# More feed-forward pairs multiplied by blocks, with their weight chunks declared up front

## The chip, the cores and the metric

One Trainium2 chip, one of its cores. The metric is the device time of one execution of the kernel, in microseconds (us). Smaller is better. Inputs lie in HBM in fp32, the output is written there in fp32.

## The reference, cut to what matters

Two layers work on 512 tokens of width 1024. In each, a modulated RMSNorm feeds two parallel branches (chunkwise retention and causal pooling), whose gated sum is projected and added to x. Then comes the feed-forward, which the change touches:

```python
mod = c_act @ w_ada[l] + b_ada[l]
sh1, sc1, g1, sh2, sc2, g2 = jnp.split(mod, N_MOD, axis=-1)
...
h2 = modulate(rmsnorm(x, norm2[l]), sh2, sc2)
gate, up = jnp.split(h2 @ w_ffn_in[l], 2, axis=-1)      # 1024 -> 2 x 2816
x = x + g2[:, None, :] * ((jax.nn.silu(gate) * up) @ w_ffn_out[l])
```

## The kernel before, in words

**Layout.** Activations are kept transposed: 128 features on the partitions, 512 tokens along the free axis. A weight unit is a block of 128x128; eight units make a chunk of 128x1024 fp32 (512 KB), the unit of loading, laid out in HBM in the order of use. A product of fp32 accuracy is made of three matmuls (`mm3`): both operands are split into a high part rounded to fp32r and a low part, the rest; high by high, low by high and high by low are summed in PSUM.

**Weight chunks.** `prep(c)` makes an ordinary chunk ready. SyncE's queue (SP) loads it into one of three `raw` tiles; `copy` writes the high part into a `w` tile, on ScalarE or VectorE; the low part goes into a second `w` tile, in one of two ways. Either VectorE or GpSimd subtracts (`nc.either`), or, for the chunks that `is_added` names, ScalarE writes the negated high part and a DMA from GpSimd's queue loads the chunk a second time and accumulates it there. There are 11 `w` tiles.

**Feed-forward.** The 2816 hidden columns are 22 tiles of 128. A *pair* i is gate tile i and up tile i: 16 units, two chunks. An ordinary pair takes 2 x 8 x 3 = 48 matmuls of 128x512. A pair *by blocks* (`seven`) treats the product as 2x2 blocks (halves of the contraction, halves of the tokens, gate and up) and makes it of seven block products in place of eight: 84 matmuls of 128x256, of the same three terms. It needs sums of blocks of the activations (tiles `x`, made once a layer) and of the weights (`seven_prep`, for each chunk): four VectorE operations of 128x256 into two kept `r` tiles, a high and a low part of 128x768 of the chunk itself, and a high and a low part of 128x512 of each of the two sums, in four `w` tiles together. Its four PSUM banks are then put together by five VectorE operations and one on ScalarE, ahead of silu, the product with up, and the split of the hidden tile. Pairs 0 to 10 are followed by a first half of `ffn_out` (11 hidden tiles), pairs 11 to 21 by the second half, where x is closed for the next norm. `background()` fetches one tile of `w_ada` (512 KB) and reduces it on VectorE, once for each ordinary pair.

**What sets the order.** The code only records operations (`Recorder.add`, so all carry the line L421). `Recorder.order` then gives each an engine, where there is a choice, and a place, from modelled costs and due times counted back from TensorE's fixed order; the engines run what it wrote down, in order. Tiles `raw`, `w` and `ps` are handed out strictly in the recorded order.

**Looking ahead.** `ahead(c)` (called for each unit) prepares chunks c to c + 2. A chunk found in the dictionary `sevens` goes to `seven_prep`, any other to `prep`. Before the change a chunk enters `sevens` only in `seven_chunk`, when its pair's turn has come. By then the look-ahead of the pair ahead has already put both chunks through `prep`; they are loaded and prepared once more by `seven_prep`, and what `prep` made of them is read by nobody. The table `SEVEN` names pairs 5, 7, 9, 11, 13, 15, 17 and 19 of each layer, so that 32 chunks are loaded twice.

Of the kernel before, what the change touches and what calls it, by code (L numbers as in the profile page):

```python
# [17 lines left out]
DEPTH = 2  # L18
# [8 lines left out]
FT = FF // P  # L27
FF_CUTS = (0, 11, FT)
EPS = 1e-6
PAD = 16  # L30
UNITS = 8
# [31 lines left out]
STAT_TILES = {"out": 4, "ffn_out": 3}  # L63
STAT_AT = 2

SEVEN = [set(range(5, FT - 1, 2))] * DEPTH
HALF_KT = KT // 2


# [363 lines left out]
def trunk(ctx, tc, xT, cin, wada, vecs, wst, rot, trid, icnt, out):  # L433


    nc = Recorder()
# [5 lines left out]
    def ps():  # L442
        return nc.tile(pp, [P, S], F32, "ps", 8)
# [7 lines left out]
    def keep(dt=F32R):  # L451
        return nc.tile(ap, [P, S], dt, "r", N_ROW)

    def weights():
        return nc.tile(wp, [P, UNITS * P], F32R, "w", N_W)

    def raw_tile():
        return nc.tile(wp, [P, UNITS * P], F32, "raw", N_RAW)
# [41 lines left out]
    order = {}  # L500
# [21 lines left out]
    sevens = {}  # L522

    def seven_chunk(l, i, k0):
        c = len(order) // UNITS
        assert len(order) % UNITS == 0
        for k, col in ((0, 0), (HALF_KT, 0), (HALF_KT, FF), (0, FF)):
            for d in range(2):
                order[(l, "ffn_in", k + k0 + d, col + i * P)] = len(order)
        sevens[c] = None  # L530
        return c

    def seven_prep(c):

        if sevens[c] is not None:
            return
        w = 2 * P
        af = raw_tile()
        nc.sync.dma_start(out=af, in_=wst[c])
        ah, al, sh, sl = (weights() for _ in range(4))  # L540
        a11, a12, a22, a21 = (af[:, n * w:n * w + w] for n in range(4))
        s34, s21 = keep(F32), keep(F32)
        nc.vector.tensor_sub(out=s34[:, :w], in0=a21, in1=a11)
        nc.vector.tensor_add(out=s21[:, :w], in0=s34[:, :w], in1=a22)
        nc.vector.tensor_add(out=s21[:, w:], in0=a21, in1=a22)
        nc.vector.tensor_sub(out=s34[:, w:], in0=a12, in1=s21[:, :w])
        copy(ah[:, :3 * w], af[:, :3 * w])
        nc.either.tensor_sub(out=al[:, :3 * w], in0=af[:, :3 * w], in1=ah[:, :3 * w].bitcast(F32))
        for n, sf in enumerate((s34, s21)):
            part = slice(n * S, n * S + S)  # L550
            copy(sh[:, part], sf)
            nc.either.tensor_sub(out=sl[:, part], in0=sf, in1=sh[:, part].bitcast(F32))
        sevens[c] = (ah, al), (sh, sl)

    def unit(l, name, k, col, n=1):
        key = (l, name, k, col)
        if key not in order:
            for q in range(n):
                order[(l, name, k, col + q * P if n > 1 else col)] = len(order)
        c, o = divmod(order[key], UNITS)  # L560
        ahead(c)
        sl = slice(o * P, (o + n) * P)
        return his[c][:, sl], los[c][:, sl]

    def ahead(c):
        for cc in range(c, c + look[0] + 1):
            if cc in sevens:
                seven_prep(cc)
            else:
                prep(cc)  # L570

    def mm3(out_ap, w, a, start, stop):

        (wh, wl), (ah, al) = w, a
        for n, (s, m) in enumerate(((wh, ah), (wl, ah), (wh, al))):
            nc.tensor.matmul(out_ap, lhsT=s, rhs=m, start=start and n == 0, stop=stop and n == 2)

    def copy(out, src):
        nc.add({"scalar": ("copy", (), dict(out=out, in_=src)), "vector": ("tensor_copy", (), dict(out=out, in_=src))})
# [7 lines left out]
    def hs(h, sl):  # L587
        return tuple(z[:, sl] for z in h)
# [87 lines left out]
    def make_h(l, which, k, sl, h, whole=None):  # L676

        hh, hl = (z[:, sl] for z in h)
        sh = mods[l][:, (0 if which == 1 else 24) + k:][:, :1]
        t = temp()[:, sl]  # L680
        nc.vector.scalar_tensor_tensor(
            out=t, in0=x[k][:, sl], scalar=gains[l, which][:, k:k + 1], in1=rs[:, sl], op0=ALU.mult, op1=ALU.mult)
        nc.add({
            "scalar": ("activation", (hh, t, AF.Identity), dict(bias=sh)),
            "vector": ("tensor_scalar", (), dict(out=hh, in0=t, scalar1=sh, scalar2=None, op0=ALU.add)),
        })
        if whole is not None:
            nc.add({
                "scalar": ("activation", (whole, t, AF.Identity), dict(bias=sh)),
                "vector": ("tensor_scalar", (), dict(out=whole, in0=t, scalar1=sh, scalar2=None, op0=ALU.add)),  # L690
            })
        nc.vector.scalar_tensor_tensor(
            out=hl, in0=t, scalar=sh, in1=hh.bitcast(F32), op0=ALU.add, op1=ALU.subtract)
# [4 lines left out]
    def first_tiles(l, which, h, name, cols, norm_b, whole=lambda k, half: None):  # L698

        o = [ps() for _ in cols]  # L700
        for sl in (A, B):
            for k in range(KT):
                for t, c in zip(o, cols):
                    mm3(t[:, sl], unit(l, name, k, c), hs(h[k], sl), k == 0, k == KT - 1)
                if sl is A and k == STAT_AT:
                    norm_b()
                    for kk in range(KT):
                        make_h(l, which, kk, B, h[kk], whole(kk, 1))
        return o
# [148 lines left out]
    for l in range(DEPTH):  # L858
# [36 lines left out]
        for g in range(2):  # L895
# [33 lines left out]
            for i in range(4):  # L929
# [4 lines left out]
                for j in range(4):  # L934
                    c0 = min(j, 2) * P
                    w = S - c0
# [94 lines left out]

        while len(order) % UNITS:
            order[("none", len(order))] = len(order)
        done = first_tiles(l, 2, h2, "ffn_in", [0, FF, P], norm_b, block)
        for k in range(HALF_KT):
            t13, t24 = temp(), temp()
# [10 lines left out]
        def seven(i):  # L1047

            cs = [seven_chunk(l, i, k0) for k0 in (0, 2)]
            o = [ps() for _ in range(4)]  # L1050
            for k in range(HALF_KT):
# [29 lines left out]
        for f, (i0, i1) in enumerate(zip(FF_CUTS, FF_CUTS[1:])):  # L1081
            hid = []
            for i in range(i0, i1):
                if i in SEVEN[l]:
                    hid.append(seven(i))
# [114 lines left out]
```

## Time and profile before

| | |
|---|---|
| median of 3 runs | 1537.04 us (1536.17 to 1537.6) |
| the profiled execution's own time | 1535.18 us |
| its span, from first to last instruction | 1533.0 us |
| granted TensorE clock, mean | 0.995 |
| DMA packets | 286.77 MB, mean 187 GB/s |
| first layer's feed-forward pairs, TensorE | 421 to 536 us (0 to 10), 596 to 712 us (11 to 21) |
| second layer's | 1167 to 1285 us, 1346 to 1461 us |

How to read what follows: PE is TensorE, PEld its weight loads, DVE VectorE, ACT ScalarE, POOL GpSimd. In a row of a group, `out<-in` names tiles without buffer numbers, then come shape, count, busy time in us, the mean length of one in ns, and the idle time of the engine ahead of it with what ended it. In a row of the timeline the first two numbers are the start and the length in us; rows that follow each other with the same operation are merged. In a row of the windows the stretch and its length are followed by each engine's busy time (and count), then the granted clock, the DMA share and GB/s. `h` and `x` as the first input of a matmul are activations and their block sums, `r` in `ffn_out` the hidden tiles, `w` the weights, `t` temporaries.

### The profile page before, as it was taken

Reading aid. Unit: us, or ns where it says so; the run is one execution under the profiler, and the core shown is the slowest. Engines: PE = TensorE matmul, PEld = TensorE weight load, DVE = VectorE, ACT = ScalarE, POOL = GpSimd, SP = SyncE. Lnnn points to the kernel's source line nnn. Section 1 sums busy time; section 2 is a strip of 40 time slices with the busy share of each in tenths; the row PEclk is TensorE's granted clock in tenths of the full one; section 3 lists DMA queues with packets and bytes.
Section 4 is the critical chain, followed back from the end, with each engine's and each line's share of the span. In section 5 each row is a group of like instructions: output and inputs, shape, how many; then the busy total and the mean of one; then the engine's idle time right before and its main releaser. Section 6 shows DMA issues by size and latency. Waiting matters only on the chain. (4 is left out here: it accounts for less than half of the span.)

```text
span 1533.0 us, 20526 instructions
## 1 busy us (share of the span) xinstructions
PE 1503.3 (98%) x7878; PEld 1287.2 (84%) x7878; DVE 1006.4 (66%) x1650; ACT 645.7 (42%) x912; POOL 300.5 (20%) x291
## 2 busy tenths in 40 slices
PE   7999999999999999999999999999999999999997
PEld 5788888888888888998888888888889888899887
DVE  8877684465568957885366768535647696478633
ACT  2377552322464412342267766322227433243332
POOL 0023151011142300222011312101211432012101
PEclk8999999999999999999999999999999999999999
DMA  7857738789694684559487865777897757444553
GB/s 259 269 158 190 161 74 255 190 246 283 149 234 153 200 251 158 170 169 279 118 221 166 202 149 134 201 180 230 251 232 182 203 167 218 124 130 159 165 125 83
DMA packets 82788, 286.77 MB, mean 187 GB/s; under 512 B 9217, under 2 KB 11521, under 8 KB 82690
## 3 DMA queue, kind: packets, MB, share of 16 engines
q1 hardware_dynamic: 64114, 217.82, 42.5%
q0 software_dynamic: 18576, 67.64, 25.1%
q8 instruction: 61, 1.00, 0.3%
q14 instruction: 37, 0.30, 0.1%
HBM read 283.33 MB, written 2.10 MB: 186 GB/s over the span
## 5 line engine op out<-in xcount | busy, mean ns | idle before, releaser
L421 PE MATMUL ps<-h,w 128*128 128x512 f32 (+1 forms) x3888 | 793.4, 362 | 8.6 <-DVE h L421 5.2
L421 PEld LDWEIGHTS ps<-h,w 128*128 128x128 f32 x3888 | 659.1, 189 | 126.2 <-DVE h L421 6.4
L421 PE MATMUL ps<-r,w 128*128 128x512 f32 (+1 forms) x2430 | 476.8, 356 | 0.1
L421 PEld LDWEIGHTS ps<-r,w 128*128 128x128 f32 x2430 | 402.3, 188 | 69.1 <-DVE r L421 0.9
L421 ACT CAST w<-raw 128x1024 fp32r<-128x1024 f32 (+2 forms) x181 | 183.3, 1013 | 346.9 <-DMA raw<-wst 190.3
L421 DVE TENSOR_TENSOR w<-raw,w 128x1024 fp32r<-128x1024 f32 (+2 forms) x162 | 206.4, 1276 | 102.5 <-PE ps L421 71.7
L421 POOL DMA_DIRECT2D w<-wst x129 | 113.6, 881 | 743.6 <-ACT w L421 690.8
L421 ACT ACTIVATE w<-w 128x1024 fp32r<-128x1024 f32 x129 | 136.6, 1060 | 200.6 <-issue 75.6
L421 DVE CAST w<-raw 128x1024 fp32r<-128x1024 f32 (+2 forms) x115 | 80.4, 699 | 169.0 <-PE ps L421 95.4
L421 DVE SCALAR_TENSOR_TENSOR raw<-raw,cact 128x1024 f32<-128x1024 f32 x96 | 122.5, 1280 | 35.0 <-DMA raw<-wada 33.9
L421 PE MATMUL ps<-x,w 128*128 128x256 f32 x768 | 96.2, 280 | 2.1 <-DVE w L421 2.1
L421 PEld LDWEIGHTS ps<-x,w 128*128 128x128 f32 x768 | 92.8, 188 | 2.5 <-DVE w L421 2.5
L421 PE MATMUL ps<-w,h 128*128 128x512 f32 x384 | 90.3, 395 | 0.0
L421 POOL TENSOR_TENSOR r<-t,r 128x512 fp32r<-128x512 f32 x48 | 79.8, 1669 | 41.1 <-ACT r L421 29.4
L421 PEld LDWEIGHTS ps<-w,h 128*128 128x128 f32 x384 | 72.0, 188 | 17.8 <-ACT r L421 0.4
L421 DVE SCALAR_TENSOR_TENSOR xall<-ps,mod,xall 128x512 f32<-128x512 f32 (+1 forms) x62 | 38.6, 629 | 72.6 <-PE ps L421 72.6
L421 ACT CAST r<-t 128x512 fp32r<-128x512 f32 (+1 forms) x106 | 65.2, 618 | 33.7 <-DVE t L421 25.7
L421 ACT ACTIVATE t<-ps 128x512 f32<-128x512 f32 x76 | 44.9, 593 | 77.8 <-PE ps L421 77.8
L421 DVE TENSOR_TENSOR t<-ps,t 128x512 f32<-128x512 f32 x76 | 51.9, 684 | 15.5 <-PE ps L421 14.6
L421 ACT COPY t<-ps 32x512 f32<-32x512 f32 (+2 forms) x88 | 47.2, 539 | 30.2 <-PE ps L421 20.6
L421 ACT ACTIVATE t<-xall 128x256 f32<-128x256 f32 (+1 forms) x44 | 21.2, 492 | 81.8 <-DVE xall L421 81.5
L421 PE MATMUL ps<-x,r 128*128 128x256 f32 (+2 forms) x256 | 52.7, 323 | 0.0
(93 smaller groups left out, 973.6 us busy)
## 6 DMA issues: line engine op xcount, KB each, us to landing
raw<-wst SPq DMA_DIRECT2D x295, 512.0 KB, 4.5
w<-wst POOLq DMA_DIRECT2D x129, 512.0 KB, 7.5
raw<-wada SPq DMA_DIRECT2D x96, 512.0 KB, 4.8
x<-rot SPq DMA_DIRECT2D x32, 256.0 KB, 7.3
xall<-xT SPq DMA_DIRECT2D x4, 512.0 KB, 5.2
out<-t SPq DMA_DIRECT2D x7, 256.0 KB, 2.2
out<-t SPq DMA_DIRECT2D x2, 128.0 KB, 2.1
tri<-trid SPq DMA_DIRECT2D x1, 128.0 KB, 4.9
```

The lines of the kernel that those rows point to most:

```text
L421: getattr(eng, method)(*[real(a) for a in args], **{k: real(v) for k, v in kw.items()})
```

## The change

Three edits. `SEVEN` names 12 pairs a layer in place of 8: 4, 5, 7, 8, 10, 11, 13, 14, 16, 17, 19 and 20, so that two pairs by blocks follow each other, then an ordinary one; pair 10, the last ahead of the first `ffn_out`, is now by blocks. When the feed-forward of a layer begins, the numbers of all its chunks by blocks are worked out and entered in `sevens`, so that the look-ahead sends them to `seven_prep` at once. In `seven_prep` the three high copies are ScalarE's; before, the planner could give them to VectorE.

```diff
-SEVEN = [set(range(5, FT - 1, 2))] * DEPTH
+SEVEN = [{4, 5, 7, 8, 10, 11, 13, 14, 16, 17, 19, 20}] * DEPTH
...
     def seven_chunk(l, i, k0):
         c = len(order) // UNITS
-        assert len(order) % UNITS == 0
+        assert len(order) % UNITS == 0 and c in sevens
...
-        sevens[c] = None
         return c
...
-        copy(ah[:, :3 * w], af[:, :3 * w])
+        nc.scalar.copy(out=ah[:, :3 * w], in_=af[:, :3 * w])
...
-            copy(sh[:, part], sf)
+            nc.scalar.copy(out=sh[:, part], in_=sf)
...
         while len(order) % UNITS:
             order[("none", len(order))] = len(order)
+        for i in SEVEN[l]:
+            c = len(order) // UNITS + 2 * i + sum(i1 - i0 for i0, i1 in zip(FF_CUTS, FF_CUTS[1:]) if i1 <= i)
+            sevens[c] = sevens[c + 1] = None
```

In the program as built, by counting its instructions: on TensorE 384 matmuls of 128x512 on `h` go, 288 of 128x256 on `h` and 384 of 128x256 on `x` come. On SyncE's queue the loads of weight chunks fall from 295 to 263, on GpSimd's the accumulating loads from 129 to 125. VectorE has 1612 instructions in place of 1556, ScalarE 972 in place of 914. The high copies of weight sums (CAST `w<-r`) stood 46 times on VectorE and 18 times on ScalarE, and now stand 96 times on ScalarE.

SyncE's queue in the second half of the first layer's feed-forward, before: between two tiles of `w_ada` (`raw<-wada`) lie the chunks of pair 13 (by blocks), of pair 14 (ordinary), and those of pair 15 as `prep` loads them in vain.

```order
L421 DMA raw_5220<-wada 128x1024
L421 DMA raw_5250<-wst 128x1024
L421 DMA raw_5273<-wst 128x1024
L421 DMA raw_5294<-wst 128x1024
L421 DMA raw_5335<-wst 128x1024
L421 DMA raw_5376<-wst 128x1024
L421 DMA raw_5413<-wst 128x1024
L421 DMA raw_5444<-wada 128x1024
```

The same place now: between the two tiles of `w_ada` lie the chunks of pairs 14 (by blocks), 15 (ordinary) and 16 (by blocks).

```order
L421 DMA raw_5318<-wada 128x1024
L421 DMA raw_5350<-wst 128x1024
L421 DMA raw_5412<-wst 128x1024
L421 DMA raw_5446<-wst 128x1024
L421 DMA raw_5504<-wst 128x1024
L421 DMA raw_5565<-wst 128x1024
L421 DMA raw_5631<-wst 128x1024
L421 DMA raw_5660<-wada 128x1024
```

Six loads carried two pairs and carry three now.

VectorE at the first chunk of pair 7, first layer, before: two low parts that nobody reads (`w_4186`, `w_4211`, of pair 7's own chunks), a tile of `w_ada`, the first step that puts pair 5 together (`t_4240`), then the chunk by blocks with all its copies (CAST) on VectorE.

```order
L421 TENSOR_TENSOR w_4186<-raw_4109,w_4159 128x1024
L421 TENSOR_TENSOR w_4211<-raw_4141,w_4196 128x1024
L421 SCALAR_TENSOR_TENSOR raw_4175,mod_0_150<-raw_4175,cact_73 128x1024
L421 TENSOR_TENSOR t_4240<-ps_4131,t_4208 128x512
L421 CAST w_4250<-raw_4201 128x768
L421 TENSOR_TENSOR w_4254<-raw_4201,w_4250 128x768
L421 TENSOR_TENSOR r_4260<-raw_4201 128x256
L421 TENSOR_TENSOR r_4264<-raw_4201 128x256
L421 TENSOR_TENSOR r_4264<-r_4260,raw_4201 128x256
L421 CAST w_4271<-r_4264 128x512
L421 TENSOR_TENSOR w_4275<-r_4264,w_4271 128x512
```

VectorE at the same chunk now: its seven operations, with two steps that put pairs 4 and 5 together (`t_4242`, `t_4292`) between them.

```order
L421 TENSOR_TENSOR r_4252<-raw_4191 128x256
L421 TENSOR_TENSOR w_4261<-raw_4191,w_4249 128x768
L421 TENSOR_TENSOR t_4242<-t_4227,ps_4068 128x256
L421 TENSOR_TENSOR r_4276<-r_4252,raw_4191 128x256
L421 TENSOR_TENSOR r_4276<-raw_4191 128x256
L421 TENSOR_TENSOR r_4252<-raw_4191,r_4276 128x256
L421 TENSOR_TENSOR t_4292<-ps_4167,t_4244 128x512
L421 TENSOR_TENSOR w_4303<-r_4276,w_4288 128x512
L421 TENSOR_TENSOR w_4303<-r_4252,w_4288 128x512
```

The copies have left VectorE's row and the two low parts in vain are gone; the steps of two pairs by blocks now lie between the operations of a third.

## The prediction

> **What bounds the kernel now.** I read the page first, then the list of TensorE's waits, then windows over single pairs of the feed-forward.
>
> ```profile
> span 1533.0 us, 20526 instructions
> PE 1503.3 (98%) x7878; PEld 1287.2 (84%) x7878; DVE 1006.4 (66%) x1650; ACT 645.7 (42%) x912; POOL 300.5 (20%) x291
> raw<-wst SPq DMA_DIRECT2D x295, 512.0 KB, 4.5
> w<-wst POOLq DMA_DIRECT2D x129, 512.0 KB, 7.5
> ```
>
> TensorE is busy for 98% of the span. So a matmul taken away is worth its time, as long as the weights still come in time; a load or a copy taken away is worth nothing by itself. TensorE's waits, longest first:
>
> ```profile
> PE ps L421 <- DVE h L421: 5.2, 1, 5.2
> ...
> PE ps L421 <- DVE w L421: 2.1, 2, 1.3
> PE ps L421 <- ACT w L421: 1.8, 3, 1.3
> PE ps L421 <- DMA w<-wst: 1.5, 2, 1.4
> ```
>
> The longest lies at the kernel's start. Waits for weights come to 5.4 us in all, of which 2.1 are on VectorE. Four neighbouring pairs of the first layer, by blocks (5), ordinary (6), by blocks (7), ordinary (8):
>
> ```profile
> core 0: us, PE busy (x) PEld busy (x) DVE busy (x) ACT busy (x) POOL busy (x), PEclk, DMA share, GB/s
> 473.36:483.25 9.89, 9.89 (x85) 9.89 (x84) 8.20 (x12) 4.82 (x6) 0.00 (x0) 1.00 0.55 179
> 483.25:494.25 11.00, 11.00 (x51) 9.02 (x49) 9.09 (x17) 3.21 (x4) 0.00 (x0) 1.00 0.64 206
> 494.25:504.14 9.89, 9.89 (x85) 9.89 (x84) 9.62 (x16) 4.25 (x7) 1.47 (x2) 1.00 0.52 169
> 504.14:515.14 11.00, 11.00 (x50) 9.02 (x49) 10.76 (x17) 4.58 (x6) 3.58 (x2) 1.00 0.55 168
> ```
>
> TensorE never stops here. A pair by blocks takes 9.89 us, an ordinary one 11.00 us. VectorE is the engine that could become late: 8.2 to 10.8 us busy in each.
>
> **Part by part: TensorE.** Eight pairs (four a layer) change from ordinary to by blocks, as the counts of the built program say. Each is worth 11.00 - 9.89 = 1.11 us, so 8 x 1.11 = **8.9 us**. All of it lies on the engine that sets the end. The matmuls come every 9.89 / 84 = 118 ns, and 11.00 / 48 = 229 ns for the long ones: two short ones cost 3% more than a long one, and seven for eight still gains 10%. [...]
>
> **VectorE.** The costs of its operations, from the groups by shape, ScalarE's price for a copy beside them:
>
> ```profile
> L421 DVE TENSOR_TENSOR w<-raw,w 128x1024 fp32r<-128x1024 f32 x128 | 170.3, 1331 | 97.7 <-PE ps L421 70.3 <-issue 13.2 <-ACT w L421 10.7
> L421 DVE SCALAR_TENSOR_TENSOR raw<-raw,cact 128x1024 f32<-128x1024 f32 x96 | 122.5, 1280 | 35.0 <-DMA raw<-wada 33.9 <-issue 0.7
> L421 DVE TENSOR_TENSOR t<-ps,t 128x512 f32<-128x512 f32 x76 | 51.9, 684 | 15.5 <-PE ps L421 14.6 <-ACT t L421 0.7
> L421 DVE TENSOR_TENSOR w<-r,w 128x512 fp32r<-128x512 f32 x61 | 43.5, 718 | 6.7 <-ACT w L421 2.5 <-PE ps L421 1.7
> L421 DVE TENSOR_TENSOR w<-raw,w 128x768 fp32r<-128x768 f32 x32 | 35.0, 1095 | 4.8 <-ACT w L421 3.1 <-PE ps L421 1.4
> L421 DVE TENSOR_TENSOR r<-t,r 128x512 fp32r<-128x512 f32 x44 | 32.5, 740 | 4.0 <-ACT r L421 3.3
> L421 DVE TENSOR_TENSOR r<-raw 128x256 f32<-128x256 f32 x64 | 31.1, 522 | 5.9 <-DMA raw<-wst 5.9
> L421 DVE CAST w<-r 128x512 fp32r<-128x512 f32 x46 | 19.7, 427 | 2.0
> L421 DVE TENSOR_TENSOR t<-t,ps 128x256 f32<-128x256 f32 x48 | 18.6, 417 | 1.0
> L421 DVE TENSOR_TENSOR t<-t,t 128x512 f32<-128x512 f32 x24 | 18.5, 769 | 0.9
> L421 DVE TENSOR_TENSOR r<-r,raw 128x256 f32<-128x256 f32 x32 | 15.6, 486 | 0.0
> L421 DVE TENSOR_TENSOR r<-raw,r 128x256 f32<-128x256 f32 x32 | 13.4, 419 | 0.1
> L421 ACT CAST w<-raw 128x768 fp32r<-128x768 f32 x29 | 24.3, 836 | 55.8 <-DMA raw<-wst 52.1 <-DVE w L421 2.9 <-PE ps L421 0.7
> L421 ACT CAST w<-r 128x512 fp32r<-128x512 f32 x18 | 10.8, 619 | 21.8 <-DVE r L421 15.0 <-PE ps L421 4.9 <-DVE w L421 1.8
> ```
>
> A chunk by blocks: 2 x 0.522 + 0.486 + 0.419 + 1.095 + 2 x 0.718 = 4.48 us, and 2 x 0.427 = 0.85 us where the high copies of the sums are VectorE's. Putting a pair together: 2 x 0.684 + 3 x 0.417 + 0.769 + 0.740 = 4.13 us. So a pair by blocks lists 2 x 4.48 + 4.13 = 13.1 us now, 14.8 before. An ordinary pair whose low parts are subtracted: 2 x 1.331 + 0.684 + 0.740 + 1.280 = 5.4 us. The two chunks prepared in vain: 2 x 1.331 = 2.7 us.
>
> Before, two pairs (20.89 us) list 14.8 + 5.4 + 2.7 = 22.9 us; the windows show 8.20 + 9.09 = 17.3 and 9.62 + 10.76 = 20.4 busy, 0.76 to 0.89 of it, since GpSimd and ScalarE take a share and starts overlap. Now three pairs (2 x 9.89 + 11.00 = 30.78 us) list 2 x 13.1 + 5.4 = 31.6 us; by the same share 24.0 to 28.1 us, 78 to 91% of the time, where it was 83 to 98%. So VectorE is on average no busier: the loads in vain and the copies given away pay for the extra pairs. Inside two neighbours by blocks it falls behind: 26.2 us listed, 19.9 to 23.3 busy, in 19.78. The 0.1 to 3.5 us must come from a lead, which the ordinary pair (11.00 us, at most 5.4 of work) builds up again.
>
> **ScalarE.** A chunk costs it 0.836 + 2 x 0.619 = 2.1 us, four chunks in 30.78 us 8.3 us; it was busy 3.2 to 4.8 us a pair. Covered. What waits there is VectorE's low part: the groups put 2.5 us on ScalarE for 61 `w<-r,w` and 3.1 for 32 `w<-raw,w`, some 0.2 us a chunk. I count nothing.
>
> **Loads.** 32 fewer on SyncE's queue and 4 fewer accumulating ones, 36 x 0.5 MB. In the four windows TensorE waits for no load, so I count zero; the most that it can give are the 1.5 us on `w<-wst`.
>
> **The waits that may go.** The two on VectorE are in the second layer, pairs 7 and 9:
>
> ```profile
> 1250.58 0.86 PE L421 MATMUL ps<-x,w 128*128 128x256 f32 x5 [0.80 <-DVE w L421]
> ...
> 1273.03 0.86 PE L421 MATMUL ps<-x,w 128*128 128x256 f32 x5 [1.28 <-DVE w L421]
> ```
> ```profile
> 1241.91 3.17 DVE L421 TENSOR_TENSOR w<-raw,w 128x768 fp32r<-128x768 f32 x1
> ```
> ```profile
> 1241.44 2.82 POOL L421 TENSOR_TENSOR w<-raw,w 128x1024 fp32r<-128x1024 f32 x1 [10.67 <-ACT w L421]
> ```
>
> VectorE's subtraction took 3.17 us in place of 1.10 while GpSimd ran one of its own, and came out 2 us late. With 1.7 us less of copies a pair these waits (0.80 + 1.28 = 2.1 us) would go; but pairs 4 and 5 now stand ahead of them, back to back. Bounds: 2.1 us gained, or as much lost again. I take half, **1.0 us** gained.
>
> **A new neighbour.** Pair 10, last ahead of the first `ffn_out`, is now by blocks, with a longer way from its last matmul to its hidden tile. Pair 9 shows that way; it ended at 515.14 + 9.89 = 525.03:
>
> ```profile
> 524.89 1.50 DVE L421 TENSOR_TENSOR t<-ps,t 128x512 f32<-128x512 f32 x2
> 526.50 1.08 DVE L421 TENSOR_TENSOR t<-t,ps 128x256 f32<-128x256 f32 x3
> 527.68 2.00 DVE L421 TENSOR_TENSOR t<-t,t 128x512 f32<-128x512 f32 x1
> 529.72 0.43 DVE L421 CAST r<-t 128x512 fp32r<-128x512 f32 x1
> 530.18 0.69 DVE L421 TENSOR_TENSOR r<-t,r 128x512 fp32r<-128x512 f32 x1
> ```
>
> The low part is done at 530.87, 5.8 us after the pair. `ffn_out` reads that tile last of 11, after 30 matmuls of 229 ns, 6.9 us. It fits by 1 us; another operation of 1.3 us in between would cost up to 0.5 us a layer. I count zero.
>
> **Sum.** 8.9 + 1.0 = 9.9 us off the profiled execution's 1535.18 (1533.0 and 2.2 around it) gives 1525.3. The median of the runs lies 1.9 us above that execution, so the forecast is 1537.04 - 9.9 = **1527.1 us**.
>
> **The rivals.** A difference under 0.2% (3.1 us) can't be told from none.
>
> *Nothing waits for weights any more* (8%): all 2.1 us on VectorE and the 1.5 on `w<-wst` go too: 8.9 + 3.6 = 12.5, **1524.5 us**. For it: fewer loads. Against: those on `w<-wst` need not lie in these pairs.
>
> *The first neighbours of a layer come late* (12%): pairs 4 and 5 begin 11 us earlier after the block sums of the activations, and three `raw` tiles feed them. VectorE falls behind by 3.5 us there in each layer: 7.0 lost, and 1.0 of old waits not regained: 8.9 - 7.0 = 1.9, **1535 us**; half of that, 3.5, gives **1531.6 us**, which I hold for twice as likely. For it: the weights' lead is short where DVE was near its limit. Against: the load of VectorE is the same per time.
>
> *VectorE becomes the bound* (4%), the one that ends slower. Ten times in the kernel two pairs by blocks stand back to back; if GpSimd holds VectorE each time as at 1241 us, and no lead is there, each costs 3.5 us: 35 - 8.9 = 26 us more, **1563 us**. It decides from 8.9 / 10 = 0.9 us lost each time. For it: the 3.17 us above. Against: in four windows TensorE lost nothing at the same load, and only 2 of 16 pairs by blocks waited. [...]
>
> *The change does not do what it says* (2%): more loads stay or the pairs don't change; then 1537. The counts of the built program speak against it.
>
> **Numbers.** The forecast itself has 74%. The range 1524.5 to 1533.5 reaches from the first rival to 5.3 us of new waits. Faster by over 0.2% means below 1534.0: 74 + 8 + 8 = 90%; within 0.2%: 4 + 2 = 6%; slower 4%.
>
> **What would show it.** Right: windows over pairs 4, 5, 7, 8 of 9.89 us each with TensorE full; no wait of TensorE on `w` above 1 us; VectorE at 78 to 91% in three pairs. Wrong: gaps ahead of matmuls on `x,w` in pairs 5, 8, 14, 17, with VectorE full before them; a gap ahead of the last hidden tile in the first `ffn_out`; or a pitch of the short matmuls other than 118 ns when two such pairs follow each other.

## The result, and the profile after

The changed kernel took 1524.45 us (median of 4 runs, 1519.62 to 1525.62), the kernel before beside it 1536.61 (4 runs, 1533.95 to 1537.6): a ratio of 0.9921, 95% interval 0.9906 to 0.9937. That is 12.2 us less; forecast were 9.9 less and 1527.1 us. Two later comparisons of the same two kernels gave 0.9932 (0.9905 to 0.9959) and 0.9928 (0.9910 to 0.9947). Over all their runs the medians are 1524.3 us (16 runs, three chips) and 1534.6 us (67 runs, four chips): **10.3 us less**; on the three chips alone it is 10.7.

The changed kernel's page, from one execution of 1525.62 us:

```profile
span 1523.9 us, 21171 instructions
...
PE 1497.8 (98%) x8166; PEld 1298.5 (85%) x8166; DVE 1019.1 (67%) x1706; ACT 660.5 (43%) x970; POOL 287.3 (19%) x285
...
raw<-wst SPq DMA_DIRECT2D x263, 512.0 KB, 4.4
w<-wst POOLq DMA_DIRECT2D x125, 512.0 KB, 7.3
```

TensorE is as full as before, with 288 matmuls more and 5.5 us less of busy time. VectorE and ScalarE work a little more in total, GpSimd less; 36 loads are gone. TensorE's waits:

```profile
PE ps L421 <- DVE h L421: 4.2, 1, 4.2
...
PE ps L421 <- DVE acc L421: 4.1, 2, 2.1
...
PE ps L421 <- ACT w L421: 0.6, 1, 0.6
PE ps L421 <- DMA w<-wst: 0.2, 1, 0.2
```

The row on VectorE's `w`, 2.1 us before, does not exist any more. The two waits on `acc`, the sums of squares at 419.7 and 774.9 us, come to 4.1 us and came to 2.7 before; in two more executions of the kernel before they come to 4.7 and 3.5 us, so the change did not bring them. Pairs 4 to 9 of the first layer (by blocks, by blocks, ordinary, twice over), in the columns of the windows in the prediction:

```profile
462.97:472.86 9.89, 9.89 (x85) 9.89 (x84) 9.48 (x16) 5.64 (x10) 2.64 (x2) 1.00 0.39 120
472.86:482.75 9.89, 9.89 (x86) 9.89 (x85) 9.77 (x18) 4.97 (x8) 0.00 (x0) 1.00 0.68 228
482.75:493.74 10.99, 10.99 (x50) 9.02 (x49) 10.55 (x19) 5.31 (x9) 3.00 (x2) 1.00 0.26 78
493.74:503.64 9.90, 9.90 (x86) 9.90 (x85) 9.90 (x14) 3.37 (x7) 5.28 (x3) 1.00 0.45 154
503.64:513.53 9.89, 9.89 (x87) 9.89 (x85) 9.30 (x16) 4.79 (x7) 1.30 (x1) 1.00 0.51 161
513.53:524.51 10.98, 10.98 (x50) 9.01 (x49) 10.76 (x21) 5.72 (x10) 1.29 (x1) 1.00 0.41 143
```

The second and third numbers of a row are equal: TensorE never stops, also not in the second of two neighbours by blocks. A pair by blocks takes 9.89 us next to another as it did alone, so each replaced pair gives 1.1 us. VectorE (the fifth number) is busy for 29.80 of 30.77 us in the first three pairs and for 29.96 of 30.77 in the next.

In this execution one stage after the other can be laid beside the kernel before. Both second halves of the feed-forward shrink by 2.25 us (175.88 to 173.63 us from start to start), which is two pairs. The second layer's first half shrinks by 5.31 us: two pairs, 2.3 us of gaps, and 0.8 us that no wait lists. The first layer's first half shrinks by only 0.7 us (115.46 to 114.75 from the matmuls on `acc` on): two pairs, less an estimated 1.7 us, half of a stretch of 3.41 us at half clock (420.46 to 423.87 us) that this execution had there and the other had not. TensorE over 119 us of the second layer's first half, before and then after:

```profile
1166.00:1285.00 119.00, 116.73 (x692) 1.00 0.66 192
```
```profile
1166.00:1285.00 119.00, 119.00 (x782) 1.00 0.55 164
```

The 2.27 us in which TensorE stood there are gone.

### The profile page after: what moved, and what is told of

The parts are those of the page before. It is cut to its first block, busy times and chain, and to the rows that moved or that the text cites. A ratio compares the mean times of both kernels' runs of the same rounds, so it can differ in the third digit from the quotient of the medians.

```text
span 1523.9 us, 21171 instructions
## 1 busy us (share of the span) xinstructions
PE 1497.8 (98%) x8166; PEld 1298.5 (85%) x8166; DVE 1019.1 (67%) x1706; ACT 660.5 (43%) x970; POOL 287.3 (19%) x285
## 4 chain that ended last, share of the span: by engine, by line
PE 89%; DVE 3%; issue 3%; DMA 3%; ACT 1%; POOL 0%; DVEq 0%; SPq 0%; POOLq 0%; ACTq 0%
PE ps L421 89%; DMA raw<-wst 2%; DVE t L421 1%; DVE w L421 1%; DVE raw L421 1%; DMA w<-wst 1%; ACT w L421 0%; POOL w L421 0%; DMA xall<-xT 0%; ACT t L421 0%; DVE r L421 0%; DVE h L421 0%; DVE acc L421 0%; ACT r L421 0%; ACT L421 0%
## 5 line engine op out<-in xcount | busy, mean ns | idle before, releaser
L421 PE MATMUL ps<-h,w 128*128 128x512 f32 (+1 forms) x3792 | 745.2, 354 | 5.3 <-DVE h L421 4.2
L421 PEld LDWEIGHTS ps<-h,w 128*128 128x128 f32 x3792 | 626.0, 190 | 107.1 <-DVE h L421 5.9
L421 ACT CAST w<-raw 128x1024 fp32r<-128x1024 f32 (+2 forms) x156 | 152.9, 980 | 216.8 <-PE ps L421 108.0
L421 DVE TENSOR_TENSOR w<-raw,w 128x1024 fp32r<-128x1024 f32 (+2 forms) x136 | 157.6, 1160 | 103.0 <-PE ps L421 89.8
L421 DVE CAST w<-raw 128x1024 fp32r<-128x1024 f32 (+1 forms) x108 | 77.6, 719 | 144.2 <-PE ps L421 93.8
L421 PE MATMUL ps<-x,w 128*128 128x256 f32 x1152 | 143.5, 279 | 0.0
L421 PEld LDWEIGHTS ps<-x,w 128*128 128x128 f32 x1152 | 139.0, 188 | 0.0
L421 ACT CAST w<-r 128x512 fp32r<-128x512 f32 x96 | 57.0, 620 | 136.5 <-DVE r L421 77.3
L421 POOL TENSOR_TENSOR r<-t,r 128x512 fp32r<-128x512 f32 x47 | 71.5, 1528 | 71.5 <-ACT r L421 54.3
L421 DVE TENSOR_TENSOR w<-r,w 128x512 fp32r<-128x512 f32 x89 | 67.4, 778 | 22.3 <-PE ps L421 12.6
```

The costliest lines, as they stand in the source:

```text
L421: getattr(eng, method)(*[real(a) for a in args], **{k: real(v) for k, v in kw.items()})
```

## The experiments

The theory was: the replaced pairs give 8.9 us on TensorE, early declaration takes away VectorE's late operands, and the extra pairs are paid for with the work that the declaration and the moved copies save. The rivals: the declaration only spares loads that were hidden anyway; VectorE becomes the bound. Later a third question came up, why executions of one kernel differ by 10 us and more. Each kernel ran beside the kernel before on the same chip.

**The changed kernel again**, without an edit.

> The changed kernel once more, beside the kernel before on the same chip. Theory A (TensorE's stream shrinks by 8.9 us, and the 2.1 us of waits on VectorE's weights go): 11 to 12 us less than before. Theory B (only the stream counts, and the rest of the first comparison was a gap in which the granted clock fell to half in one execution and not in the other): 8.9 us less on average, with single executions some 1.7 us apart for each such dip.

1524.01 us (6 runs), ratio 0.9932 (0.9905 to 0.9959), 10.4 us less: between the two theories, and the interval holds both. The profiled execution took 1529.57, and showed a wait that the first profile had not: 1.47 us in the first `ffn_out`, on pair 10's hidden tile.

**Declaration alone**: the changed kernel with the old pairs, its copies given back to the planner (the run "Pairs and declaration" below restores the copies in the same way).

```diff
-SEVEN = [{4, 5, 7, 8, 10, 11, 13, 14, 16, 17, 19, 20}] * DEPTH
+SEVEN = [set(range(5, FT - 1, 2))] * DEPTH
...
-        nc.scalar.copy(out=ah[:, :3 * w], in_=af[:, :3 * w])
+        copy(ah[:, :3 * w], af[:, :3 * w])
...
-            nc.scalar.copy(out=sh[:, part], in_=sf)
+            copy(sh[:, part], sf)
```

> The declaration alone: 8 pairs a layer as before, copies by the planner as before, but no chunk prepared twice. Theory A (the two waits in the second layer came from VectorE's work in vain): they are gone, 2 us less than before, ratio 0.9985. Rival (loads and work in vain were hidden, the waits come from GpSimd holding VectorE): no difference, ratio 1.000.

1532.04 us, ratio 0.9982 (0.9969 to 0.9995; 12 runs), 2.4 us under the median of the kernel before on that chip. TensorE over the same stretch of the second layer:

```profile
1166.00:1285.00 119.00, 119.00 (x700) 1.00 0.63 182
```

No gap is left there. So something that came with the loads in vain held TensorE up. Two subtractions in vain on VectorE are gone; but so is GpSimd's subtraction of 2.82 us that ran beside VectorE's of 3.17 us at 1241 us (the prediction shows both rows). It stands at that place in all four traces that have the gaps, and neither here nor in the next run, which have none. The rival, that GpSimd holds VectorE, is therefore not ruled out: the two causes were not parted. The size of the gain in time is less sure than the gap (see the two pitches below: this execution had the faster one in its first layer).

**Copies alone**: the kernel before with the three high copies on ScalarE.

```diff
-        copy(ah[:, :3 * w], af[:, :3 * w])
+        nc.scalar.copy(out=ah[:, :3 * w], in_=af[:, :3 * w])
...
-            copy(sh[:, part], sf)
+            nc.scalar.copy(out=sh[:, part], in_=sf)
```

> The copies on ScalarE alone: 8 pairs a layer, chunks still prepared twice. Theory A (VectorE's lateness in the second layer costs 2.4 us, and 1.7 us less of copies a pair is enough to end it): 1 to 2.4 us less than before, ratio 0.9985 to 0.9993. Rival (only the work in vain matters): ratio 1.000, the waits on VectorE's weights at pairs 7 and 9 of the second layer still there.

1532.34 us, ratio 0.9995 (0.9978 to 1.0011; 12 runs): no difference that can be measured. In its trace the gaps are gone too:

```profile
1166.00:1285.00 119.00, 118.98 (x712) 1.00 0.69 201
```

Either edit alone ends the same 2 us of gaps, so their gains don't add up.

**Pairs alone**: the kernel before with the new table, so that 48 chunks are loaded late, and twice.

```diff
-SEVEN = [set(range(5, FT - 1, 2))] * DEPTH
+SEVEN = [{4, 5, 7, 8, 10, 11, 13, 14, 16, 17, 19, 20}] * DEPTH
```

> 12 pairs alone: copies by the planner, chunks still prepared twice. Listed for VectorE in three pairs: 2 x 14.8 + 5.4 + 2 x 2.7 = 40.4 us, by the share of 0.76 to 0.89 30.7 to 36.0 us busy in 30.78. Theory A (VectorE has just enough room after the change and not without the declaration): TensorE waits up to 5 us in three pairs, eight times over 20 us, so between 9 us less and 12 us more than before, I expect about 0. Rival (VectorE is nowhere near its limit): 9 us less, ratio 0.994.

1568.74 us, ratio 1.0221 (1.0196 to 1.0246), 34 us slower and worse than either theory had said. Its waits:

```profile
PE ps L421 <- DVE w L421: 19.2, 13, 5.2
PE ps L421 <- ACT w L421: 7.9, 5, 4.4
...
PE ps L421 <- DMA w<-wst: 5.1, 4, 3.3
```

This is the rival "VectorE becomes the bound", in full: 13 waits on its `w`. The first long one opens pair 5, and VectorE's row just ahead of it shows what is in the way:

```profile
476.96 2.71 PE L421 MATMUL ps<-h,w 128*128 128x256 f32 x11 [5.20 <-DVE w L421]
```
```profile
470.12 2.92 DVE L421 TENSOR_TENSOR r<-raw 128x256 f32<-128x256 f32 x2
472.97 1.48 DVE L421 TENSOR_TENSOR r<-r,raw 128x256 f32<-128x256 f32 x1
474.48 0.43 DVE L421 TENSOR_TENSOR r<-raw,r 128x256 f32<-128x256 f32 x1
474.82 2.08 DVE L421 TENSOR_TENSOR w<-raw,w 128x1024 fp32r<-128x1024 f32 x2
476.83 1.28 DVE L421 TENSOR_TENSOR w<-r,w 128x512 fp32r<-128x512 f32 x2
```

The chunk's sums begin at 470.12, when TensorE has been at pair 4 for nine microseconds. Of the two subtractions merged at 474.82 the first writes a low part that nobody reads, by the program's tiles, and the second is what TensorE waits for: the work in vain stands right ahead of the work that is late. The three rows of waits on weights come to 32.2 us, 26.8 more than in the kernel before. TensorE also works for 25.3 us at half clock around them (mean granted clock 0.987, 0.995 in the kernel before), which costs an estimated half of that, 12.7. Less 8.9 us for the pairs, that makes 30.6 of the 34 us.

**Pairs and declaration**, copies by the planner.

> 12 pairs and the declaration, but copies by the planner, who may give them to VectorE. Theory A (the declaration pays for the pairs, the copies matter little): within 1.5 us of the changed kernel, ratio to before 0.992 to 0.993. Rival (the copies on ScalarE carry it: 1.7 us a pair of VectorE): 3 to 8 us slower than the changed kernel.

1526.56 us, ratio 0.9946 (0.9929 to 0.9963; 12 runs). So with 12 pairs the declaration is worth 42 us, and the table without it loses. The moved copies add about 2.5 us (1524.01 on that chip), between the two theories, which these intervals don't separate from nothing.

**Copies on VectorE**: the changed kernel with all three high copies given to VectorE.

```diff
-        nc.scalar.copy(out=ah[:, :3 * w], in_=af[:, :3 * w])
+        nc.vector.tensor_copy(out=ah[:, :3 * w], in_=af[:, :3 * w])
...
-            nc.scalar.copy(out=sh[:, part], in_=sf)
+            nc.vector.tensor_copy(out=sh[:, part], in_=sf)
```

> The changed kernel with the three high copies of a chunk by blocks all on VectorE. Listed for VectorE: 2 x (0.556 + 2 x 0.427) = 2.8 us more a pair, so 2 x 15.9 + 5.4 = 37.2 us in three pairs, by the share 28.3 to 33.1 busy in 30.78. Theory A (VectorE's time decides): 0 to 2.3 us of waits in three pairs, some 6 us over the changed kernel in all, ratio to before about 0.997. Rival (the place of the copies does not matter): ratio 0.993 as the changed kernel.

1536.77 us, ratio 1.0023 (1.0008 to 1.0038): the whole gain is gone, 12 us over the changed kernel's 1524.3 on other chips.

```profile
PE ps L421 <- DMA w<-wst: 6.1, 6, 3.2
...
PE ps L421 <- DVE w L421: 4.5, 7, 1.1
...
PE ps L421 <- ACT w L421: 2.3, 2, 1.4
```

VectorE had no room for the copies (busy for 69.33 of 71.00 us from 463 to 534 us); besides its own `w` the accumulating loads come late too. The three rows come to 12.9 us, where the changed kernel's first profile has 0.8; what of them is due to which was not separated.

**Seventeen pairs**: the changed kernel with pairs 4 to 20 all by blocks, no ordinary pair between.

```diff
-SEVEN = [{4, 5, 7, 8, 10, 11, 13, 14, 16, 17, 19, 20}] * DEPTH
+SEVEN = [set(range(4, FT - 1))] * DEPTH
```

> The changed kernel with every pair from 4 to 20 by blocks, 17 a layer, none ordinary between them. The stream gains 10 x 1.11 = 11 us more. Theory A (a pair by blocks keeps VectorE 10.0 to 11.7 us busy in 9.89, and without ordinary pairs it never catches up): 0.1 to 1.8 us lost a pair, 3 to 60 us in 34 pairs, less a lead of some 5 us a half; I expect the gain eaten, 1520 to 1535 us, with waits on VectorE's weights growing along each half. Rival (VectorE has room left): 11 us under the changed kernel, ratio to before 0.986.

1562.32 us, ratio 1.0197 (1.0174 to 1.0221), slower than both theories had allowed.

```profile
PE ps L421 <- DMA w<-wst: 20.9, 7, 8.7
PE ps L421 <- DVE w L421: 11.9, 19, 1.8
```

TensorE's matmuls alone would be 11 us shorter than the changed kernel's (10 pairs by 1.11), but without the ordinary pair, in which the lead is built up again, there are 19 waits on VectorE and 7 on accumulating loads, of 32.8 us together, and TensorE works for 13.2 us at half clock around them (mean granted clock 0.989), which costs an estimated half of that, 6.6. The kernel is 38 us slower than the changed one's 1524.3 on other chips. Without any ordinary pair the gain is lost; how many are needed was not tried.

**STAT_AT 4**: the changed kernel, with the matmuls that finish the second token half's sums of squares (`acc`) two contraction tiles later in TensorE's order. It was aimed at the two waits on `acc`.

```diff
-STAT_AT = 2
+STAT_AT = 4
```

> The changed kernel with STAT_AT 4 in place of 2: 45 matmuls of the first half of tokens in place of 27 go ahead of the second half's sum of squares, on which TensorE waits 2.2 us at each of two changes of stage, in most executions with the clock at half for 3.4 us behind it. Theory A (those waits are the cause of the dips and both are lost time): 2 x 2.2 us of waits and 1.7 us for each dip less, 4 to 8 us under the changed kernel, no half clock near 420 and 775 us. Rival (the wait only moves to the second half's first matmuls): no difference, dips as before.

1519.77 us (6 runs), ratio 0.9920 (0.9899 to 0.9942), an interval that also holds the changed kernel's ratios. Once more, on another chip and beside the next two kernels:

> The changed kernel with STAT_AT 4, once more, to stand beside the others on one chip. If its gain is real: 3 to 5 us under the changed kernel on this chip and 13 to 15 us under the kernel before. If the difference of the earlier call was one of chips or of executions: within 1.5 us of the changed kernel.

1515.4 us (6 runs, 1509.25 to 1522.21), ratio 0.9872 (0.9845 to 0.9899), where the changed kernel as it is ran there at 1524.16. It beats both kernels. The place at 420 us, in the changed kernel and then in this one:

```profile
419.66 0.70 PE L421 MATMUL ps<-acc,ones 128*128 128x256 f32 x2 [2.06 <-DVE acc L421]
```
```profile
419.23 0.59 PE L421 MATMUL ps<-acc,ones 128*128 128x256 f32 x2
```

The wait is gone. Together the two places can give 4.1 us, and an estimated 3.4 more where half clock follows, half of 3.41 us at each; 9 us needs another source.

**STAT_AT 4 in the kernel before**, the same line.

> The kernel before with STAT_AT 4 in place of 2, nothing else. Theory A (the waits of 2.1 to 2.5 us on the accumulated sums at 420 and 775 us, and the stretches at half clock that follow them in some executions, belong to the stages' starts and not to the change): the same 3 to 5 us go here as went from the changed kernel, so 1529 to 1532 us where the kernel before stands at 1534 to 1535; no wait on the sums above 1 us. Theory B (they hurt only beside the early loads of the change): within 1 us of the kernel before.

1535.61 us, ratio 1.0006 (0.9994 to 1.0018): nothing. Theory A falls here. The wait has only moved, to the last tiles of `h` for the second half, 11 us later:

```profile
431.43 2.89 PE L421 MATMUL ps<-h,w 128*128 128x256 f32 x11 [2.14 <-ACT h L421]
```

In this kernel three `r` activations stand on ScalarE ahead of the last ones of `h`, in the changed one with STAT_AT 4 only one. Its gaps in the second layer remain as well (2.9 us on VectorE's `w`).

**Another pair in place of pair 10**, on top of STAT_AT 4.

```diff
-SEVEN = [{4, 5, 7, 8, 10, 11, 13, 14, 16, 17, 19, 20}] * DEPTH
+SEVEN = [{3, 4, 6, 7, 9, 11, 13, 14, 16, 17, 19, 20}] * DEPTH
```

> The changed kernel with STAT_AT 4 and, in each layer, pairs 3, 4, 6, 7, 9 by blocks in the first half in place of 4, 5, 7, 8, 10; the second half as changed. Pair 10 is ordinary. Theory A (pair 10 by blocks makes its hidden tile late for the first ffn_out, 1.6 to 2.4 us in some executions): 1 to 3 us under e7_again, with no wait on the hidden tile at 541 to 545 us. Theory B (that wait is exchanged for one on the weights of pairs 3 and 4, which begin 11 us earlier after the sums of the activations): the same as e7_again or up to 4 us over it, with gaps on w in pairs 3 and 4.

1521.85 us (4 runs), ratio 0.9912 (0.9894 to 0.9929): not better, some 6 us over the run with STAT_AT 4 that stood beside it. The wait on the hidden tile does not appear in its trace, but two others on VectorE's `w` do, in pairs 3 and 4 of the second layer (0.41 us at 1202.1, 0.96 at 1208.6). That is theory B's mechanism, and more than its 4 us. About half of the difference is the pitch of the short matmuls, which the paragraphs below explain: the profiled execution had the faster one in 10 of its 24 pairs by blocks, that of the run beside it in all 24, worth 5.3 of the 10.5 us between the two. An ordinary pair ahead of `ffn_out` did not pay here.

**The changed kernel a third time.**

> The changed kernel as it is, to have more executions of it beside the kernel before. If the forecast's sum is right and the base of three runs was high: 9 to 11 us under the kernel before, ratio 0.993 to 0.994. If all waits on weights went as well: 12 us or more, ratio 0.992 or less.

1524.16 us (6 runs), ratio 0.9928 (0.9910 to 0.9947): 11.6 us under that chip's median of the kernel before, a little more than the forecast's sum and less than the 12 us of the other case.

**Two pitches.** The profiled execution of that run had pairs 4 and 5 like this:

```profile
462.54:472.06 9.52, 9.52 (x86) 9.52 (x84) 9.11 (x15) 4.52 (x8) 2.66 (x2) 1.00 0.31 110
472.06:481.58 9.52, 9.52 (x87) 9.52 (x85) 9.40 (x16) 5.11 (x9) 0.00 (x0) 1.00 0.60 191
481.58:492.56 10.98, 10.98 (x50) 9.02 (x49) 10.88 (x19) 4.82 (x9) 3.00 (x2) 1.00 0.38 124
```

The same program, the same full clock (1.00), no gap, and 9.52 us in place of 9.89: 113.3 ns a short matmul in place of 117.8. The ordinary pair, of long matmuls, takes 10.98 as ever. The pitch holds over a stage: here through both halves of the first layer, from pair 4 (462 us) to 760 us. To see whether this belongs to the execution or to the kernel, two more profiled executions of each kernel:

> The kernel before, one more profiled execution. Theory A (the 128x256 matmuls have two pitches, 117.8 and 113.3 ns, and which one holds in a stage is a matter of the execution): some half of a feed-forward may stand at 113.3 here too, and the time is about 1535.2 less 4.5 ns for each of the 1344 short matmuls of pairs by blocks that ran at 113.3, plus 1.7 us for each stretch at half clock behind a short gap, within 2 us. Theory B (only kernels whose chunks are declared early get the faster pitch in the feed-forward): 117.8 ns in all four halves and 1533 to 1538 us.

> As p1_before: theory A allows any mix of the two pitches, with the time following the count; theory B has 117.8 ns in all four halves.

> The changed kernel, one more profiled execution. Theory A: the time is about 1525.6 (its first profile, 117.8 ns in all four halves, two stretches at half clock in the feed-forward) less 4.5 ns for each of the 2016 short matmuls of pairs by blocks that ran at 113.3, 9.1 us at most, plus or minus 1.7 for each stretch at half clock more or less, plus what pair 10's hidden tile waits, within 2 us. Rival: the spread of executions has another source, and the time doesn't follow that count.

> As p3_after: the time follows the count of short matmuls at 113.3 ns and of the stretches at half clock within 2 us, or, by the rival, it does not.

They took 1536.22 and 1533.77 us (before), 1524.46 and 1522.85 (after). The second of the kernel before has the faster pitch too, in its last half, from 1347 to 1513 us; the first three pairs there, without declared chunks:

```profile
1347.21:1356.73 9.52, 9.52 (x85) 1.00 0.51 165
1356.73:1367.72 10.99, 10.99 (x51) 1.00 0.42 145
1367.72:1377.24 9.52, 9.52 (x86) 1.00 0.51 164
```

So the faster pitch does not need declared chunks, and theory B falls. By the rule put down beforehand (theory A, the times in the same order) the four come to 1536.9, 1533.3, 1523.5 and 1522.5 us: each is met within 1 us, but only the second had a half at the faster pitch. Another thing that differs is the clock behind the wait on `acc`. The 10 us from 417 to 427, in the kernel before and in its next execution:

```profile
417.00:427.00 10.00, 7.71 (x64) 1.00 0.58 129
```
```profile
417.00:427.00 10.00, 7.71 (x51) 0.83 0.57 134
```

The kernel before stands still for the same 2.29 us both times; once the clock stays at 1.00, once it falls to half for 3.41 us. I count half of that as lost, 1.7 us, an estimate: the second row has 13 matmuls fewer, 1.5 us at 117.8 ns. All profiled executions of the two kernels, and of the one with STAT_AT 4 (halves in order of time; the clock's stretches without those of the start and the end):

| execution | us | halves at 113.3 ns | stretches at half clock | waits on VectorE's `w`, us | wait for pair 10's hidden tile, us |
|---|---|---|---|---|---|
| before | 1535.18 | none | 0 | 2.1 | |
| before | 1536.22 | none | 1 | 2.1 | |
| before | 1533.77 | 4th | 0 | 2.5 | |
| after | 1525.62 | none | 2 | none | none |
| after | 1524.46 | none | 0 | none | 1.28 |
| after | 1522.85 | none | 0 | none | 0.28 |
| after | 1523.91 | 1st, 2nd | 3 | none | 1.81 |
| after | 1529.57 | 1st | 3 | none | 1.47 |
| STAT_AT 4 | 1516.22 | 1st, 2nd | 0 | none | none |
| STAT_AT 4 | 1509.25 | all | 0 | none | none |

Adding 4.5 ns for each of the 420 or 588 matmuls of a half at the faster pitch and taking off 1.7 us a stretch and the last column, the five executions of the changed kernel come to 1522.2, 1523.2, 1522.6, 1521.5 and 1524.9: 3.4 us apart, where they were 6.7. The time follows the count within 2 us, as theory A had it. The two executions with STAT_AT 4 come to 1520.8 and 1518.3, 2 to 5 us under the changed kernel's mean of 1522.9: that much can be STAT_AT's own, and the rest of what parts 1509.25 from the changed kernel is the pitch.

## Why the prediction was right or wrong, point by point

**The time.** Measured 1524.45, 0.05 us below the range's low end of 1524.5. The difference was right: -9.9 forecast; -10.3 from the medians of 16 and 67 runs, -9.8 between the means of the five and the three profiled executions (1525.28 and 1535.06). The step that failed is the last of the sum: "The median of the runs lies 1.9 us above that execution, so the forecast is 1537.04 - 9.9". That median was of three runs. Over 67 runs the kernel before lies between 1528.13 and 1540.12, with a median of 1534.6: 0.6 us below the profiled execution that I corrected away from, in place of 1.9 above it, and 2.5 us under the base that I used. From 1534.6 the same sum gives 1524.7. In the first comparison by itself, on one chip, the kernel before stood at 1536.61 and the difference was 12.2 us; its interval, 9.7 to 14.4 us, holds 9.9 as well, so four runs a side cannot say whether base or difference was off there. That it was the base rests on the later comparisons. The second fault is the range: its low end was made from one rival, with nothing for the spread of the executions.

**The replaced pairs, 8.9 us**: right, on a condition that I did not see. The pitch was 118 ns in both first profiles, next to another pair by blocks as well, and each half shrank by two pairs of 1.11. "Wrong" was to be "a pitch of the short matmuls other than 118 ns", and executions with 113.3 do occur. There a replaced pair gives 11.00 - 9.52 = 1.48 us, 11.8 for eight, and the 16 old ones give 0.37 each. A row of the kernel before had shown it already, in 120 short matmuls of another stage:

```profile
L421 PE MATMUL ps<-r,w 128*128 128x256 f32 x120 | 13.8, 276 | 0.0
```

One of them is listed with 276 ns there, 279 elsewhere in that trace; their starts lie 113.3 ns apart. I had read the pitch from one place.

**The waits that may go, 1.0 us**: mis-sized. "I take half": all went, 2.1 to 2.5 us in three executions before, none in five after; declaration alone does it, the copies alone too; whether VectorE's own work or GpSimd beside it made the operands late stays open. The fear that pairs 4 and 5 would cost the lead did not come true: TensorE waits for no VectorE weight there. What is left of waits on `w` in the five executions is ScalarE's, 0.6 to 2.9 us, all within the first 67 us, and the few on loads below.

**A new neighbour, zero**: mis-sized the other way, by 0 to 1.8 us (1.0 in the mean). It is the gap ahead of the last hidden tile that was named as a sign of being wrong, but for another reason than the one weighed. I followed VectorE's chain, which fits by 1 us, and thought of one more operation there. What comes late is a load. The execution of 1523.91 us, ScalarE:

```profile
537.05 1.05 ACT L421 CAST w<-raw 128x1024 fp32r<-128x1024 f32 x1 [7.21 <-DMA raw<-wst]
538.14 1.06 ACT L421 ACTIVATE w<-w 128x1024 fp32r<-128x1024 f32 x1
539.10 0.61 ACT L421 ACTIVATE t<-t 128x512 f32<-128x512 f32 x1
```

VectorE and TensorE in the same execution:

```profile
539.75 0.69 DVE L421 TENSOR_TENSOR t<-t,t 128x512 f32<-128x512 f32 x1 [3.98 <-ACT t L421]
```
```profile
540.96 6.26 PE L421 MATMUL ps<-r,w 128*128 128x512 f32 x18 [1.81 <-DVE r L421]
```

Pair 10's silu (`t<-t`) stands on ScalarE behind a copy that waits 7.21 us for its chunk; VectorE's product waits for the silu, TensorE for the hidden tile. In the first profile the copy began 3.8 us earlier, and there was no wait:

```profile
533.29 1.05 ACT L421 CAST w<-raw 128x1024 fp32r<-128x1024 f32 x1 [2.50 <-DMA raw<-wst]
534.38 1.06 ACT L421 ACTIVATE w<-w 128x1024 fp32r<-128x1024 f32 x1
535.54 0.63 ACT L421 ACTIVATE t<-t 128x512 f32<-128x512 f32 x1
```

What differs is the order of two loads, of the copy's chunk on SyncE's queue and of an accumulating load on GpSimd's. Two rows of the timeline in the first profile, then two in the execution of 1523.91 us:

```profile
527.87 0.33 SPq L421 DMA_DIRECT2D raw<-wst  x1
528.19 0.88 POOL L421 DMA_DIRECT2D w<-wst  x1 [1.44 <-ACT w L421]
```
```profile
528.02 0.88 POOL L421 DMA_DIRECT2D w<-wst  x1 [0.78 <-ACT w L421]
528.35 0.33 SPq L421 DMA_DIRECT2D raw<-wst  x1
```

Issued 0.32 us ahead of the accumulating load, the chunk landed 5.4 us later; issued 0.33 us behind it, 8.7 us later. It is so in all eight traces: issued ahead, 4.9 to 5.6 us and no wait (first profile, both with STAT_AT 4); issued behind, 7.6 to 9.3 us and a wait of 0.28 to 2.26 us (the other four of the changed kernel, and the run of pairs and declaration). No run changed this order by itself, so it is a correlation, though one without exception.

So the two small terms, +1.0 and 0, came out as about +2.2 and -1.0. Their sum was right by luck.

**ScalarE, "covered"**: by its time, yes (3.4 to 5.7 us a pair in the windows above). But in the rows above the silu behind the copy that waited 7.21 us began at 539.10, 3.56 us later than in the first profile, and with it TensorE waited 1.81 us.

**VectorE at 78 to 91%**: wrong, it was 97% in both groups of three pairs. Two things were missing. I had counted one reduction of a `w_ada` tile for an ordinary pair, 1.28 us; between 463 and 534 us, with two ordinary pairs, there are six, and longer ones:

```profile
L421 DVE SCALAR_TENSOR_TENSOR raw<-raw,cact 128x1024 f32<-128x1024 f32 x6 | 10.6, 1768 | 0.0
...
L421 DVE TENSOR_TENSOR r<-raw 128x256 f32<-128x256 f32 x16 | 10.6, 676 | 0.5 <-DMA raw<-wst 0.5
```

And single operations stretch, as the second row shows: 676 ns in place of 522. It cost nothing, since the ordinary pairs give the lead back, but it leaves no room: with the copies on VectorE, without the declaration or without the ordinary pairs TensorE waits at once.

**Loads, zero**: right within 1 us; the waits on `w<-wst` were 1.5, 0 and 0.4 us in three executions before, 0.2 in four of five after and 1.1 in the fifth.

**The rivals.** "Nothing waits for weights any more" (1524.5 us) is half true: nothing on VectorE, and pair 10 instead; of the 1.5 us on `w<-wst`, 1.35 lay at 777.9 us, outside these pairs. "The first neighbours come late" did not happen. "VectorE becomes the bound" (1563 us) did not happen here, but it is what the change's parts do one by one: 1568.74 us for the pairs alone.

**What stays open**: what starts the faster pitch, and why 6 of 8 halves with STAT_AT 4 had it and only 3 of 20 of the changed kernel as it is. What ends it can be seen in part. In the execution of 1523.91 us, from 751 to 759 us, ahead of the two matmuls on `acc` at 759.8, and from 761 to 768, behind them:

```profile
L421 PE MATMUL ps<-r,w 128*128 128x256 f32 x73 | 8.4, 276 | 0.0
```
```profile
L421 PE MATMUL ps<-r,w 128*128 128x256 f32 x61 | 7.3, 279 | 0.0
```

By the starts of single matmuls, a stretch at the faster pitch met the matmuls on `acc` 14 times in the traces of all runs, and each time the slower one followed them. So the pitch is not chance alone; why these two matmuls end it is not shown. Of the second layer's first half 0.8 us are in no listed wait; 0.5 of them lie in the kernel before's pairs 7 and 9, which took 2.6 us longer there than pair 5 of the first layer for the same matmuls, with waits of 2.1.

## What to carry to other kernels

A forecast is a difference and a base, and each has its own error: three runs gave a base 2.5 us above the median of 67, more than two of the pairs that were being counted are worth. Where an engine is nearly full, price parts of a change together: the pairs alone lost 34 us, the declaration alone won 2, both together won 8, and 10 with the copies moved. And follow a late result through every queue that it passes: here the silu stood behind a copy that waited 7.21 us for its load, and TensorE waited 1.81 us for what came of it.

## What the runs showed of the hardware

The streams of 128x256 matmuls with a weight load each had two pitches at full clock (1.00): 117.8 ns (84 in 9.89 us, first profile) and 113.3 ns (84 in 9.52 us, execution of 1523.91 us). Which one held changed within an execution: the faster one stayed for up to 330 us (1161 to 1489 us in the execution of 1509.25 us) and ended all 14 times at the matmuls on `acc` where it met them, in the first profile before at 1154.9 us and in the first one after at 405.1 us. The 128x512 matmuls kept 229 ns beside both (48 in 11.00 and 10.98 us).

The clock fell to half for 3.41 us (0.83 in the mean over 10 us) after TensorE had stood still, mostly for only 1.8 to 2.5 us, in some executions and not in others of the same kernel: after 2.29 us in the kernel before once and once not. In the first profile after, the short matmuls started 213 ns apart in such a stretch (granted clock 0.50 from 420.46 to 423.87 us). With longer stops it was half for 6.83 us (a stop of 5.20 us in the pairs alone, 0.93 in the mean from 463 to 534 us) or 10.24 us (8.69 us with seventeen pairs). What sets these lengths, and why the same stop has it once and once not, no run shows.
